# Strassen column tiles in a hybrid encoder trunk: ACT's and DVE's programs held in a written order, weight forms cast six products ahead

## The chip, the core and the metric

The kernel runs on one core of one Trainium2 chip. The metric is device time in microseconds, the median of repeated runs; one further execution was profiled. TensorE (PE) multiplies matrices, ScalarE (ACT) copies, rounds and evaluates functions, VectorE (DVE) adds and multiplies element by element, GpSimd (POOL) does a little of the rest, and SyncE (SP) issues the transfers from HBM. Each engine has a program of its own and runs it in order; semaphores tie them together.

## The reference

Two layers, 512 tokens of width 1024, float32. Each layer is a SwiGLU feed-forward block, a three-branch token mixer and a second SwiGLU block, each between RMSNorms, with residuals:

```python
def swiglu_ffn(h, w_gate, w_up, w_down):
    return (jax.nn.silu(h @ w_gate) * (h @ w_up)) @ w_down
...
for l in range(DEPTH):          # DEPTH = 2, D_MODEL = 1024, D_FF = 2816
    h = rms_norm(x, norm_pre[l, 0])
    x = x + 0.5 * rms_norm(swiglu_ffn(h, ffn1_w_gate[l], ffn1_w_up[l], ffn1_w_down[l]), norm_post[l, 0])
    h = rms_norm(x, norm_pre[l, 1])
    m = hybrid_mixer(h, ...)
    x = x + rms_norm(m, norm_post[l, 1])
    h = rms_norm(x, norm_pre[l, 2])
    x = x + 0.5 * rms_norm(swiglu_ffn(h, ffn2_w_gate[l], ffn2_w_up[l], ffn2_w_down[l]), norm_post[l, 2])
```

The change lies in the gate and up projections of the feed-forward blocks, so it is met four times in a run.

## The kernel before

**Precision.** A float32 operand is split into a high part, rounded by ACT to the matmul's format (a cast, `whi` for weights), and a low part, which DVE makes by subtracting (`wlo`). Each product of two operands is three matmuls: high by high, high by low, low by high.

**A feed-forward block** (`ffn`) has d_ff = 22 column tiles of 128. Tiles 0 and 1 are computed by tokens (bank `pf`) and turned, tile 2 in the plain way: `pg` and `pu` are its gate and up projections, DVE's product into `hid[2]` (L450) ends it. Meanwhile `forms.finish` splits the forms T1 to T4 of the activations. Tiles 3 to 21, 19 of them, go through `unit`: the gate and up columns of one tile are the two columns of a 2x2 block product (contraction halves by token halves) that is done by Strassen's scheme in Winograd's form with seven products instead of eight. Then `out_proj` multiplies by `w_down`.

**One tile.** The raw weights are four blocks of 128 x 512 in a buffer `raw` of five places (three such buffers); place 4 and in turn places 1, 0 and 2 are overwritten by four DVE sums (`add`, L348). The seven weight forms are cast and their low parts subtracted, two neighbouring forms by one DVE instruction where they can be paired. `whi` and `wlo` are rings of five buffers of two forms each. A product is 12 matmuls of 256 columns: 4 contraction chunks by 3. In order, with the bank each adds into:

| product | weight form | activation form | bank | afterwards |
|---|---|---|---|---|
| 0 | A11 | B11 | A | ACT copies A to p1 (L372) |
| 1 | S3 | T3 | C | ACT copies C to p7 (L380) |
| 2 | S2 | T2 | A | ACT copies A to u2 (L382) |
| 3 | A12 | B21 | B | DVE adds B and p1 into hid (L348) |
| 4 | S1 | T1 | A | ACT copies A to u4 (L392) |
| 5 | A22 | T4 | C | DVE subtracts u2 and u4 (L394, L395) |
| 6 | S4 | B22 | A | Silu of hid and of A (L399, L400), product into hid (L401) |

Bank A runs on through products 0, 2, 4 and 6, so each of them must wait until ACT has copied what the last one left there; between two of them lies one product into another bank.

**What sets the order.** TensorE's instructions are held in the order in which they are written (`mm` calls `tc.keep_in_program_order`). Everything on ACT, DVE and SP is placed by a scheduler, which fills each engine's program by what it reckons will be ready, the earlier written first; it can therefore move work of a later tile, of the forms or of the down projection ahead of what is written before it. The two Silus and the last product of a tile are written, by the argument `before`, after the third product of the next one.

Of the kernel before, what the change touches and what calls it, by code (L numbers as in the profile page):

```python
# [8 lines left out]
F32 = mybir.dt.float32  # L9
F32R = mybir.dt.float32r  # L10
AF = mybir.ActivationFunctionType
ALU = mybir.AluOpType

P = 128
D = 1024
# [4 lines left out]
NF = DFF // P  # L20
# [21 lines left out]
def kernel(  # L42
# [9 lines left out]
    nc = tc.nc  # L52
# [5 lines left out]
    wp = ctx.enter_context(tc.tile_pool(name="wp", bufs=5))  # L58
    tp = ctx.enter_context(tc.tile_pool(name="tp", bufs=1))
    gp = ctx.enter_context(tc.tile_pool(name="gp", bufs=2))  # L60
# [4 lines left out]
    def mm(*a, **k):  # L65
        tc.keep_in_program_order(nc.tensor.matmul(*a, **k))  # L66

    def transpose(*a):
        tc.keep_in_program_order(nc.tensor.transpose(*a))

    def slot(name, dt=F32, tag="t"):
        return tp.tile([P, 512], dt, tag=tag, name=name, bufs=SLOTS[tag])

    def bank(n, tag="pb"):
        return psp.tile([P, 512], F32, tag=tag, name=n, bufs=BANKS[tag])
# [9 lines left out]
    for c in range(2):  # L85
        blk = strict[:, c * CHUNK:(c + 1) * CHUNK]
        r = slice(c * CHUNK, (c + 1) * CHUNK)
# [68 lines left out]
    def load_kcols(w2d, c0, width):  # L156

        nk = 1024 // width
        v = lambda r: r.rearrange("p (k c) -> p k c", c=width)
        out_ = []  # L160
        for k0 in range(0, KC, nk):
            hi, lo = load_w([(v, w2d[k0 * P:(k0 + nk) * P, c0:c0 + width].rearrange("(k p) c -> p k c", p=P))], 1024)
            out_ += [(v(hi)[:, k], v(lo)[:, k]) for k in range(nk)]
        return out_
# [111 lines left out]
    class Forms:  # L276


        def __init__(self):
            self.first = []  # L280
            self.raw = None
            self.parts = {}
# [28 lines left out]
            for n, k0, t0 in (("B11", 0, 0), ("B21", 4, 0), ("B22", 4, 256)):  # L311
                self.parts[n] = [(xh[:, k0 + k, t0:t0 + 256], xl[:, k0 + k, t0:t0 + 256]) for k in range(4)]

    class Ring:


        def __init__(self):
            self.n = 0

        def put(self, src):  # L320

            two = len(src.shape) == 3
            if self.n % 2 == 0:
                self.hi, self.lo = (wp.tile([P, 1024], F32R, tag=t, name=t).rearrange("p (f c) -> p f c", f=2)
                                    for t in ("whi", "wlo"))
            h = self.n % 2
            assert not (two and h)
            self.n += 2 if two else 1
            f = slice(0, 2) if two else slice(h, h + 1)
            src = src if two else src.unsqueeze(1)  # L330
            for j in range(f.start, f.stop):
                nc.scalar.copy(self.hi[:, j], src[:, j - f.start])  # L332
            nc.vector.tensor_tensor(self.lo[:, f], src, self.hi[:, f].bitcast(F32), op=ALU.subtract)  # L333
            v = lambda t: t.rearrange("p (k c) -> p k c", c=P)
            r = [(v(self.hi[:, j]), v(self.lo[:, j])) for j in range(f.start, f.stop)]
            return r if two else r[0]

    H0, H1 = slice(0, 256), slice(256, 512)

    def unit(w0, w1, c0, forms, ring, h, before):  # L340


        r = wp.tile([P, 5, 512], F32, tag="raw", name="raw", bufs=3)
        for w, q0 in ((w0, 0), (w1, 1)):
            for j in range(2):
                nc.sync.dma_start(r[:, q0 + 2 * j].rearrange("p (k c) -> p k c", c=P),  # L346
                                  w[j * 512:(j + 1) * 512, c0:c0 + P].rearrange("(k p) c -> p k c", p=P))
        add = lambda o, a, b: nc.vector.tensor_tensor(o, a, b, op=ALU.add)  # L348
        add(r[:, 4], r[:, 1], r[:, 3])
        add(r[:, 1], r[:, 1], r[:, 0])  # L350
        A, B, C = bank("A"), bank("B"), bank("C")

        def product(w, n, ps, first):
            wh, wl = w
            for k, (fh, fl) in enumerate(forms.parts[n]):
                for j, (a, b) in enumerate(((wh, fh), (wh, fl), (wl, fh))):
                    mm(ps[:, H0], a[:, k], b, start=(first and k == 0 and j == 0), stop=False, skip_group_check=True)

        cp = gp.tile([P, D], F32, tag="g", name="cp")
        p1, p7, u2, u4 = (cp[:, j * 256:(j + 1) * 256] for j in range(4))  # L360
        put = ring.put
        even = ring.n % 2 == 0
        if even:
            a11, s3 = put(r[:, 0:2])
            add(r[:, 0], r[:, 4], r[:, 0])
            s2, a12 = put(r[:, 0:3:2])
        else:
            a11 = put(r[:, 0])
            add(r[:, 0], r[:, 4], r[:, 0])
            s2, s3 = put(r[:, 0:2])  # L370
        product(a11, "B11", A, True)
        nc.scalar.copy(p1, A[:, H0])  # L372
        if even:
            add(r[:, 2], r[:, 2], r[:, 0])
            a22, s1 = put(r[:, 3:5])
        else:
            a12, s1 = put(r[:, 2:5:2])
            add(r[:, 2], r[:, 2], r[:, 0])
        product(s3, "T3", C, True)
        nc.scalar.copy(p7, C[:, H0])  # L380
        product(s2, "T2", A, False)
        nc.scalar.copy(u2, A[:, H0])  # L382
        if before is not None:
            before()
        if even:
            s4 = put(r[:, 2])
        else:
            s4, a22 = put(r[:, 2:4])
        product(a12, "B21", B, True)
        add(h[:, H0], B[:, H0], p1)  # L390
        product(s1, "T1", A, False)
        nc.scalar.copy(u4, A[:, H0])  # L392
        product(a22, "T4", C, False)
        nc.vector.tensor_tensor(u2, C[:, H0], u2, op=ALU.subtract)  # L394
        nc.vector.tensor_tensor(u4, p7, u4, op=ALU.subtract)  # L395
        product(s4, "B22", A, False)

        def after():
            nc.scalar.activation(h[:, H0], h[:, H0], AF.Silu)  # L399
            nc.scalar.activation(h[:, H1], A[:, H0], AF.Silu)  # L400
            nc.vector.tensor_tensor(h, cp[:, 512:1024], h, op=ALU.mult)  # L401

        return after


    def ffn_weights(wg, wu):
# [5 lines left out]
    def ffn(wg, wu, wd, weights, forms, arrive, finish, upcoming, early, late, begin):  # L412

        if begin is None:
            wgt, wut = weights
        else:
            wgt = load_kcols(wg, 0, 256)
            begin(0)
            wut = load_kcols(wu, 0, 256)
            begin(1)  # L420
            arrive[0]()
        hk = []
        for i in range(NT):
            pf = bank("pf", "pb")
            mm_tok(pf[:, 0:256], i, wgt)
            if i + 1 < NT:
                arrive[i + 1]()
            mm_tok(pf[:, 256:512], i, wut, first=False)
            h = slot("ht", tag="s")
            nc.scalar.activation(h[:, 0:256], pf[:, 0:256], AF.Silu)  # L430
            nc.vector.tensor_tensor(h[:, 0:256], pf[:, 256:512], h[:, 0:256], op=ALU.mult)
            hk.append(h)
        hid = [None] * NF
        ring = Ring()

        def turn(f):
            pt = bank("pth", "pa")
            for i in range(NT):
                transpose(pt[:, i * P:(i + 1) * P], hk[i][:, f * P:(f + 1) * P], ident)
            hid[f] = slot("hid", tag="q")  # L440
            nc.scalar.copy(hid[f], pt)

        pg = proj_cols(wg, 2 * P, "pg")
        turn(0)
        turn(1)
        forms.finish()
        pu = proj_cols(wu, 2 * P, "pu")
        hid[2] = slot("hid")
        nc.scalar.activation(hid[2], pg, AF.Silu)
        nc.vector.tensor_tensor(hid[2], pu, hid[2], op=ALU.mult)  # L450
        spare.clear()
        last = None
        for f in range(3, NF):
            hid[f] = slot("hid", tag="t" if f < 18 else "q")
            last = unit(wg, wu, f * P, forms, ring, hid[f], last)
        last()
        late()

        def stat(f):
            sh, sl = slot("sh", F32R, "s"), slot("sl", F32R, "s")  # L460
            split(sh, sl, hid[f])
            return sh, sl

        return out_proj(wd, NF, stat, TAIL, finish, upcoming, early)
# [507 lines left out]
    g0 = load_g(norm_pre[0, 0])  # L972
    forms = form0 = Forms()
    arrive = [pre_norm(0, g0, forms=forms)]

    def begin(n):
        if n == 0:
            load_x(1)
            arrive.append(pre_norm(1, g0, forms=form0))
        else:  # L980
            load_x(2)
            load_x(3)
            arrive.extend(pre_norm(i, g0, forms=form0) for i in (2, 3))
# [3 lines left out]
    for idx, (l, s) in enumerate(subs):  # L987
# [10 lines left out]
        here, forms = forms, Forms() if s != 0 else None  # L998
# [11 lines left out]
        if idx + 1 < len(subs):  # L1010
            l1, s1 = subs[idx + 1]
# [39 lines left out]
```

## Time and profile before

| | us |
|---|---|
| runs shown: median of 3 | 2421.8 |
| lowest, highest | 2421.22, 2428.5 |
| profiled execution, its own time | 2428.07 |
| its span, first to last instruction | 2426.4 |
| PE busy | 2361.9 (97%) |
| DVE busy | 1620.8 (67%) |
| ACT busy | 1123.7 (46%) |
| mean granted TensorE clock | 0.997 |

How to read the profile's lines. A group's line gives source line, engine, operation, what is written from what, shape and count, then busy us and mean ns of one, then the engine's idle time ahead of the group and what ended it. A line of waits gives who waited for whom, the total in us, how many times, and the longest. A timeline's line gives start and duration in us, and in brackets the idle time before it and its releaser. A window's line gives each engine's busy time in a stretch, the granted clock and the share of the DMA engines. Matmuls are pipelined: 0.28 us is the modelled passage of one of 256 columns, while the next starts sooner. Most matmuls and nearly all casts go through one-line helpers, so the names (`A<-xh,whi`) tell more than the lines.

### The profile page before, as it was taken

What the parts mean: (1) busy time and instruction counts of PE and PEld (TensorE: products, weight loads), DVE (VectorE), ACT (ScalarE), POOL (GpSimd) and SP (SyncE); (2) the same over time, 40 slices, a digit from 0 to 9 for tenths busy, and PEclk for the clock granted to TensorE, in tenths of its full rate; (3) what the DMA queues carried; (4) which work ended last, traced back from release to release, by engine and by line L of the source; (5) the groups of instructions that cost most, each with busy time, mean ns of one, the idle gap of its engine ahead of it and who ended that gap; (6) DMA issues with size and microseconds to landing.
All of it is one profiled execution on the core that took longest, in us unless ns stands there. A gap on an engine that the chain in (4) does not pass through costs nothing. (4 is left out here: it accounts for less than half of the span.)

```text
span 2426.4 us, 35901 instructions
## 1 busy us (share of the span) xinstructions
PE 2361.9 (97%) x14264; PEld 2100.7 (87%) x14264; DVE 1620.8 (67%) x2329; ACT 1123.7 (46%) x2148; POOL 176.3 (7%) x287
## 2 busy tenths in 40 slices
PE   8999999999999999999999999999999999999998
PEld 7999888887888899998899998888878888999987
DVE  7777436859965497774387774378599644877733
ACT  6555426644323365553365553366333334555522
POOL 0000002201011100000000000012010211000000
PEclk9999999999999999999999999999999999999999
DMA  5333423231333233333233333241313332333331
GB/s 167 105 88 105 137 89 97 70 92 53 106 91 101 79 87 98 95 112 131 70 88 101 92 114 130 70 114 54 107 53 105 87 104 71 96 96 96 124 102 45
DMA packets 307160, 231.74 MB, mean 96 GB/s; under 512 B 11722, under 2 KB 284140, under 8 KB 306992
## 3 DMA queue, kind: packets, MB, share of 16 engines
q1 hardware_dynamic: 306992, 229.46, 31.9%
q8 instruction: 111, 1.82, 0.3%
q14 instruction: 57, 0.47, 0.1%
HBM read 227.32 MB, written 2.10 MB: 95 GB/s over the span
## 5 line engine op out<-in xcount | busy, mean ns | idle before, releaser
L106 DVE TENSOR_TENSOR wlo<-raw,whi 128x1024 fp32r<-128x1024 f32 (+1 forms) x266 | 333.6, 1258 | 236.1 <-ACT whi L105 229.0
L105 ACT CAST whi<-raw 128x1024 fp32r<-128x1024 f32 (+1 forms) x266 | 278.1, 1046 | 397.2 <-PE gate L66 122.6
L332 ACT CAST whi<-raw 128x512 fp32r<-128x512 f32 x532 | 323.8, 620 | 237.0 <-PE A L66 102.0
L333 DVE TENSOR_TENSOR wlo<-raw,whi 128x1024 fp32r<-128x1024 f32 (+1 forms) x304 | 330.5, 1087 | 68.7 <-ACT whi L332 65.3
L348 DVE TENSOR_TENSOR raw<-raw 128x512 f32<-128x512 f32 x304 | 203.8, 688 | 121.2 <-DMA raw<-in_ffn_w_up_dram 118.5
L66 PE MATMUL o<-whi,sh 128*128 128x512 f32 x704 | 274.2, 389 | 0.0
L66 PE MATMUL o<-wlo,sh 128*128 128x512 f32 x704 | 273.9, 389 | 0.0
L66 PE MATMUL o<-whi,sl 128*128 128x512 f32 x704 | 273.9, 389 | 0.0
L66 PE MATMUL A<-xh,whi 128*128 128x256 f32 x608 | 176.5, 290 | 43.8 <-ACT cp L392 43.7
L106 DVE TENSOR_TENSOR sl<-hid,sh 128x512 fp32r<-128x512 f32 x88 | 60.4, 690 | 193.8 <-ACT sh L105 193.8
L66 PE MATMUL A<-xh,wlo 128*128 128x256 f32 x608 | 173.4, 285 | 0.0
L66 PE MATMUL A<-xl,whi 128*128 128x256 f32 x608 | 173.4, 285 | 0.0
L641 DVE SCALAR_TENSOR_TENSOR y<-u,cw,y 128x511 f32<-128x511 f32 (+14 forms) x240 | 164.3, 747 | 0.0
L105 ACT CAST sh<-hid 128x512 fp32r<-128x512 f32 x88 | 54.5, 624 | 233.3 <-PE o L66 232.4
L66 PEld LDWEIGHTS A<-xh,whi 128*128 128x128 f32 x608 | 117.8, 194 | 50.1 <-ACT cp L392 49.8
L66 PEld LDWEIGHTS o<-whi,sl 128*128 128x128 f32 x704 | 132.1, 188 | 27.5
L66 PEld LDWEIGHTS o<-wlo,sh 128*128 128x128 f32 x704 | 132.2, 188 | 27.3
L66 PEld LDWEIGHTS o<-whi,sh 128*128 128x128 f32 x704 | 132.2, 188 | 27.1
L66 PE MATMUL gate<-xh,whi 128*128 128x512 f32 x384 | 151.3, 394 | 0.0
L66 PE MATMUL gate<-xl,whi 128*128 128x512 f32 x384 | 149.6, 390 | 0.0
L66 PE MATMUL gate<-xh,wlo 128*128 128x512 f32 x384 | 149.5, 389 | 0.0
L193 POOL TENSOR_TENSOR rs<-ms,mhalf 128x1 f32<-128x1 f32 x48 | 31.0, 646 | 1510.3 <-DVE ms L191 1510.3
(280 smaller groups left out, 6231.3 us busy)
## 6 DMA issues: line engine op xcount, KB each, us to landing
raw<-in_w_in_dram SPq DMA_DIRECT2D x108, 512.0 KB, 4.3
raw<-in_ffn_w_down_dram SPq DMA_DIRECT2D x88, 512.0 KB, 4.4
raw<-in_ffn_w_gate_dram SPq DMA_DIRECT2D x152, 256.0 KB, 3.3
raw<-in_ffn_w_up_dram SPq DMA_DIRECT2D x152, 256.0 KB, 4.5
raw<-in_w_branch_dram SPq DMA_DIRECT2D x24, 512.0 KB, 3.9
raw<-in_w_out_dram SPq DMA_DIRECT2D x16, 512.0 KB, 4.4
raw<-in_ffn_w_gate_dram SPq DMA_DIRECT2D x12, 512.0 KB, 5.3
raw<-in_ffn_w_up_dram SPq DMA_DIRECT2D x12, 512.0 KB, 4.1
```

What stands on the lines that cost most here:

```text
L66: tc.keep_in_program_order(nc.tensor.matmul(*a, **k))
L105: nc.scalar.copy(hi, src)
L106: nc.vector.tensor_tensor(lo, src, hi.bitcast(F32), op=ALU.subtract)
L193: nc.gpsimd.tensor_tensor(rs, ms, mhalf[:, 0:1], op=ALU.pow)
L332: nc.scalar.copy(self.hi[:, j], src[:, j - f.start])
L333: nc.vector.tensor_tensor(self.lo[:, f], src, self.hi[:, f].bitcast(F32), op=ALU.subtract)
L348: add = lambda o, a, b: nc.vector.tensor_tensor(o, a, b, op=ALU.add)
L641: nc.vector.scalar_tensor_tensor(y[:, back:], u[:, :S - back], cw[:, c, j:j + 1], y[:, back:], op0=ALU.mult, op1=ALU.add)
```

## The change

`unit` and its helper `Ring` are replaced by `block_tiles`, which writes the 19 tiles as one sequence of 133 products. A step `g` holds, in this order: on ACT the copies or Silus after product g-1 (`taken`); on PE product g; on DVE the sums and on ACT the cast for product g+6, then on DVE its low part (`prepare`; a pair's low part comes with the second form); on DVE what follows product g-1 (`summed`). Six steps with only `prepare` stand ahead of product 0. Each instruction on ACT and DVE is passed to `tc.keep_in_program_order`, which puts it behind the instruction that was traced last on its engine; loads on SP aren't held. The raw weights of tile u+2 are asked for where the first form of tile u+1 is prepared. The forms keep to the ring of five buffers, and pairs never cross a tile's end: an even tile has the pairs (0,1), (2,3), (4,5) and 6 alone, an odd one 0 alone and (1,2), (3,4), (5,6). Where the second form of a pair lies before the first in `raw`, both are addressed in reverse. The slots for `hid` are all named ahead of the sequence.

```diff
-    def unit(w0, w1, c0, forms, ring, h, before):
...
+    PRODUCTS = (("B11", 0), ("T3", 2), ("T2", 0), ("B21", 1), ("T1", 0), ("T4", 2), ("B22", 0))
+
+    PLACES = (0, 1, 0, 2, 4, 3, 2)
+    AHEAD = 6
+
+    def block_tiles(w0, w1, fs, forms, hid):
+
+        pin = tc.keep_in_program_order
+        copy = lambda o, i: pin(nc.scalar.copy(o, i))
+        silu = lambda o, i: pin(nc.scalar.activation(o, i, AF.Silu))
+        tt = lambda o, a, b, op: pin(nc.vector.tensor_tensor(o, a, b, op=op))
...
+        def low(g0, g1):
+
+            hi, lo = ring[g0 // 2]
+            q0, q1 = PLACES[g0 % 7], PLACES[g1 % 7]
+            r, h = raw[g0 // 7], g0 % 2
+            if g0 == g1:
+                sub(lo[:, h], r[:, q0], hi[:, h].bitcast(F32))
+            elif q0 < q1:
+                sub(lo, r[:, q0:q1 + 1:q1 - q0], hi.bitcast(F32))
+            else:
+                sub(lo[:, ::-1], r[:, q1:q0 + 1:q0 - q1], hi[:, ::-1].bitcast(F32))
+
+        def prepare(g):
+
+            u, j = divmod(g, 7)
+            r = raw[u]
+            if j == 0:
+                add(r[:, 4], r[:, 1], r[:, 3])
+                add(r[:, 1], r[:, 1], r[:, 0])
+            if j == 2:
+                add(r[:, 0], r[:, 4], r[:, 0])
+            if j == 5:
+                add(r[:, 2], r[:, 2], r[:, 0])
...
+            copy(ring[g // 2][0][:, g % 2], r[:, PLACES[j]])
+            if g % 2 and j:
+                low(g - 1, g)
+            elif g % 2 or j == 6:
+                low(g, g)
...
+        def taken(g):
...
+            if j == 0:
+                copy(p1, A[:, H0])
...
+            if j == 4:
+                copy(u4, A[:, H0])
+            if j == 6:
+                silu(h[:, H0], h[:, H0])
+                silu(h[:, H1], A[:, H0])
+
+        def summed(g):
...
+            if j == 3:
+                add(h[:, H0], B[:, H0], p1)
+            if j == 5:
+                sub(u2, C[:, H0], u2)
+                sub(u4, p7, u4)
+            if j == 6:
+                tt(h, cps[u][:, 512:1024], h, ALU.mult)
+
+        for g in range(-AHEAD, n + 1):
+            f = g + AHEAD
+            if f % 7 == 0 and f < n:
+                if f == 0:
+                    load(0)
+                if f // 7 + 1 < len(fs):
+                    load(f // 7 + 1)
+            if 0 < g:
+                taken(g - 1)
+            if 0 <= g < n:
+                product(g)
+            if f < n:
+                prepare(f)
+            if 0 < g:
+                summed(g - 1)
...
         spare.clear()
-        last = None
         for f in range(3, NF):
             hid[f] = slot("hid", tag="t" if f < 18 else "q")
-            last = unit(wg, wu, f * P, forms, ring, hid[f], last)
-        last()
+        block_tiles(wg, wu, list(range(3, NF)), forms, hid)
         late()
```

More of the change, by code (lines that the diff above doesn't have):

```diff
@@ L312, in finish @@
                 self.parts[n] = [(xh[:, k0 + k, t0:t0 + 256], xl[:, k0 + k, t0:t0 + 256]) for k in range(4)]
[L314 to L336, printed above, removed]
@@ L338 @@
-    H0, H1 = slice(0, 256), slice(256, 512)
-    def unit(w0, w1, c0, forms, ring, h, before):
[L343 to L403, printed above, removed]
@@ new lines, with load, product, parts @@
+    H0, H1 = slice(0, 256), slice(256, 512)
+    PRODUCTS = (("B11", 0), ("T3", 2), ("T2", 0), ("B21", 1), ("T1", 0), ("T4", 2), ("B22", 0))
[6 more added lines that the diff above has]
+        tt = lambda o, a, b, op: pin(nc.vector.tensor_tensor(o, a, b, op=op))
+        add = lambda o, a, b: tt(o, a, b, ALU.add)
+        sub = lambda o, a, b: tt(o, a, b, ALU.subtract)
+        n = 7 * len(fs)
+        raw, banks, cps, ring = {}, {}, {}, {}
+        def load(u):
+            r = wp.tile([P, 5, 512], F32, tag="raw", name="raw", bufs=3)
+            for w, q0 in ((w0, 0), (w1, 1)):
+                for j in range(2):
+                    nc.sync.dma_start(r[:, q0 + 2 * j].rearrange("p (k c) -> p k c", c=P),
+                                      w[j * 512:(j + 1) * 512, fs[u] * P:(fs[u] + 1) * P]
+                                      .rearrange("(k p) c -> p k c", p=P))
+            raw[u] = r
+        def low(g0, g1):
[18 more added lines that the diff above has]
+                add(r[:, 2], r[:, 2], r[:, 0])
+            if g % 2 == 0:
+                ring[g // 2] = [wp.tile([P, 1024], F32R, tag=t, name=t).rearrange("p (f c) -> p f c", f=2)
+                                for t in ("whi", "wlo")]
+            copy(ring[g // 2][0][:, g % 2], r[:, PLACES[j]])
[3 more added lines that the diff above has]
+                low(g, g)
+        def product(g):
+            u, j = divmod(g, 7)
+            name, b = PRODUCTS[j]
+            if j == 0:
+                banks[u] = [bank(x) for x in "ABC"]
+                cps[u] = gp.tile([P, D], F32, tag="g", name="cp")
+            ps = banks[u][b][:, H0]
+            hi, lo = (t[:, g % 2].rearrange("p (k c) -> p k c", c=P) for t in ring[g // 2])
+            first = j in (0, 1, 3)
+            for k, (fh, fl) in enumerate(forms.parts[name]):
+                for m, (a, b_) in enumerate(((hi, fh), (hi, fl), (lo, fh))):
+                    mm(ps, a[:, k], b_, start=(first and k == 0 and m == 0), stop=False, skip_group_check=True)
+        def parts(u):
+            cp = cps[u]
+            return [cp[:, x * 256:(x + 1) * 256] for x in range(4)], hid[fs[u]], banks[u]
+        def taken(g):
+            u, j = divmod(g, 7)
+            (p1, p7, u2, u4), h, (A, B, C) = parts(u)
+            if j == 0:
+                copy(p1, A[:, H0])
+            if j == 1:
+                copy(p7, C[:, H0])
+            if j == 2:
+                copy(u2, A[:, H0])
+            if j == 4:
[4 more added lines that the diff above has]
+        def summed(g):
+            u, j = divmod(g, 7)
+            (p1, p7, u2, u4), h, (A, B, C) = parts(u)
+            if j == 3:
[20 more added lines that the diff above has]
+                summed(g - 1)
@@ L433, in ffn @@
         hid = [None] * NF
-        ring = Ring()
         def turn(f):
```

## The prediction

> **What bounds the kernel now.** I read the page's busy lines first, then the list of waits, then the windows of the four Strassen stages, then the timeline of one stall and of one stage start.
>
> ```profile
> PE 2361.9 (97%) x14264; PEld 2100.7 (87%) x14264; DVE 1620.8 (67%) x2329; ACT 1123.7 (46%) x2148; POOL 176.3 (7%) x287
> ```
> ```profile
> DVE raw L348 <- DMA raw<-in_ffn_w_up_dram: 118.5, 65, 3.1
> ACT hid L399 <- DVE hid L348: 89.7, 56, 3.0
> PE A L66 <- ACT cp L392: 43.7, 28, 2.2
> ```
> ```profile
> core 0: us, PE busy (x) PEld busy (x) DVE busy (x) ACT busy (x) POOL busy (x), PEclk, DMA share, GB/s
> 52.40:258.40 206.00, 195.48 (x1598) 193.52 (x1596) 155.46 (x223) 115.71 (x248) 0.00 (x0) 0.99 0.34 101
> 890.80:1096.40 205.60, 193.61 (x1598) 191.96 (x1597) 155.22 (x224) 116.05 (x248) 0.00 (x0) 1.00 0.35 102
> 1255.10:1459.20 204.10, 193.63 (x1597) 191.89 (x1596) 155.04 (x223) 116.09 (x248) 0.00 (x0) 1.00 0.35 102
> 2094.30:2300.20 205.90, 195.03 (x1597) 193.37 (x1597) 155.59 (x224) 115.91 (x248) 0.00 (x0) 0.99 0.35 102
> sum 821.60, PE 777.75 PEld 770.74 DVE 621.30 ACT 463.75 POOL 0.00; mean PE 194.44 PEld 192.68 DVE 155.33 ACT 115.94 POOL 0.00
> ```
>
> TensorE is the bound nearly everywhere; its largest wait in the whole run is 43.7 us, on the copy of u4 (L392), in the stages that the change rewrites. Now one stall, first TensorE:
>
> ```profile
> 80.97 0.28 PE L66 MATMUL C<-T4l,whi 128*128 128x256 f32 x1
> 81.09 0.28 PE L66 MATMUL C<-T4h,wlo 128*128 128x256 f32 x1
> 82.66 0.39 PE L66 MATMUL A<-xh,whi 128*128 128x256 f32 x1 [1.29 <-ACT cp L392]
> 82.88 0.28 PE L66 MATMUL A<-xl,whi 128*128 128x256 f32 x1
> ```
>
> Matmuls start every 0.12 us, so a tile of 84 takes 10.08 us and a stage of 19 tiles 1596 x 0.12 = 191.5 us; four take 766.1 where the windows sum to 821.6. So 55.5 us are lost. The stall begins at 81.21 and ends at 82.66 (1.45), and the second matmul comes 0.10 late: 0.26 more than the row's 1.29. So 28 stalls are 43.7 + 28 x 0.26 = 51.0 of the 55.5. Who is late, on DVE and ACT:
>
> ```profile
> 78.19 1.42 DVE L348 TENSOR_TENSOR raw<-raw 128x512 f32<-128x512 f32 x2 [2.73 <-DMA raw<-in_ffn_w_up_dram]
> 79.53 1.22 DVE L333 TENSOR_TENSOR wlo<-raw,whi 128x1024 fp32r<-128x1024 f32 x1
> 80.66 0.42 DVE L348 TENSOR_TENSOR hid<-B,cp 128x256 f32<-128x256 f32 x1
> 81.00 0.68 DVE L348 TENSOR_TENSOR raw<-raw 128x512 f32<-128x512 f32 x1
> 82.36 1.23 DVE L333 TENSOR_TENSOR wlo<-raw,whi 128x1024 fp32r<-128x1024 f32 x1 [0.68 <-ACT whi L332]
> ```
> ```profile
> 81.11 0.42 ACT L399 ACTIVATE hid<-hid 128x256 f32<-128x256 f32 x1 [2.04 <-DVE hid L348]
> 81.71 0.62 ACT L332 CAST whi<-raw 128x512 fp32r<-128x512 f32 x1 [0.18 <-DVE raw L348]
> 82.24 0.37 ACT L392 COPY cp<-A 128x256 f32<-128x256 f32 x1
> 82.50 0.62 ACT L332 CAST whi<-raw 128x512 fp32r<-128x512 f32 x1
> ```
>
> DVE stands 2.73 us before weight sums for a later tile whose transfer has not landed; the sum into hid is queued behind it, ACT's Silu waits for that, a cast waits for another sum, and u4's copy, whose data were ready long before, comes last. It is a fault of the order on the two engines, not of their load. The rest of the 55.5 is mostly two stretches at half clock (below) and small gaps.
>
> **The change, part by part.** (a) *Same work.* Matmuls, casts, sums and transfers stay in number and size: per tile 4 weight sums, 7 casts, 3 paired and 1 single low part. Some paired subtractions read their halves in reverse. No row shows a reversed pair; a contiguous one takes 1.22 us, bounds zero and, as two singles of 0.60, nothing either. I take zero.
>
> (b) *Weights six products ahead.* The low part of product 6 of a tile is now cast while the tile's product 0 runs, so the raw buffer comes free about 8.6 us earlier and the load of the tile three on has more than a tile to land. The 118.5 us of DVE waits on transfers go; the transfers keep to SP's queue, with nothing new ahead of them.
>
> (c) *The copies out of PSUM first in each step.* u4's copy, queued in the step behind product T1, stands behind casts of earlier steps alone. Does that hold at full pace? I walked the written order for all 19 tiles, with these prices:
>
> ```profile
> L333 DVE TENSOR_TENSOR wlo<-raw,whi 128x1024 fp32r<-128x1024 f32 x54 | 66.0, 1222 | 18.6 <-ACT whi L332 18.1
> L348 DVE TENSOR_TENSOR raw<-raw 128x512 f32<-128x512 f32 x67 | 44.8, 688 | 27.2 <-DMA raw<-in_ffn_w_up_dram 26.6
> L394 DVE TENSOR_TENSOR cp<-C,cp 128x256 f32<-128x256 f32 x19 | 7.9, 418 | 0.4 <-PE C L66 0.4
> ```
> ```profile
> 84.17 1.22 DVE L333 TENSOR_TENSOR wlo<-raw,whi 128x1024 fp32r<-128x1024 f32 x1
> 85.31 0.69 DVE L401 TENSOR_TENSOR hid<-cp,hid 128x512 f32<-128x512 f32 x1
> 85.91 0.69 DVE L348 TENSOR_TENSOR raw<-raw 128x512 f32<-128x512 f32 x1
> ```
>
> Back to back, DVE starts its next after 1.14 us for a pair (84.17 to 85.31), 0.60 for 512 columns, 0.33 for 256; ACT after 0.53 for a cast (81.71 to 82.24) and 0.26 for a copy. DVE's tile is 4 x 0.60 + 3 x 1.14 + 0.60 + 3 x 0.33 + 0.60 = 8.0 of 10.08 us, ACT's about 5.5. A handoff costs 0.03 us (81.00 + 0.68 to ACT at 81.71; 81.71 + 0.62 to DVE at 82.36), so does a wait of DVE for its own result (two sums of 0.69 in 1.42), and ACT or DVE starts 0.20 us after a product's last matmul slot. In the walk the weights lie ready 3.7 us early or more. The copies do not. The tightest chain is in an odd tile, where product 0 starts at 0, product k at 1.44 k, and the forms of the next tile are made. The last Silu of the tile before:
>
> ```profile
> L400 ACT ACTIVATE hid<-A 128x256 f32<-128x256 f32 x18 | 6.9, 381 | 6.5 <-PE A L66 6.5
> ```
>
> It runs 0.20 to 0.58; behind it the cast of S4 0.48 to 1.10; DVE's low pair 1.13 to 2.36, the product into hid 2.28 to 2.97, the sums of r4 and r1 2.88 to 3.57 and 3.61 to 4.30; the cast of S3 4.33 to 4.95, its low pair 4.98 to 6.21, r0's sum 6.24 to 6.93, the casts of S2 and A12 6.97 to 8.11; and only then u4's copy, 8.01 to 8.38, though product 4 ended at 7.20. Product 6 starts at 8.64: 0.2 us to spare. In even tiles u2's copy has the same 0.2, behind the cast of S3. Each tile's chain starts anew from TensorE's own end, so nothing piles up. I take no stall in steady state, by a hair. Below that price there is nothing; above, a stage of the old order took 206.0 us for 19 tiles, 21.7 us for two.
>
> (d) *The start of a stage.* Each held instruction goes behind whatever was traced last on its engine. For DVE that is the product into hid[2] (L450), which needs all of pu:
>
> ```profile
> 39.45 1.22 DVE L333 TENSOR_TENSOR wlo<-raw,whi 128x1024 fp32r<-128x1024 f32 x1
> 40.70 0.69 DVE L348 TENSOR_TENSOR raw<-raw 128x512 f32<-128x512 f32 x1
> ...
> 52.62 0.69 DVE L450 TENSOR_TENSOR hid<-pu,hid 128x512 f32<-128x512 f32 x1 [0.69 <-PE pu L66]
> ```
> ```profile
> 52.19 0.39 PE L66 MATMUL pu<-xh,wlo 128*128 128x512 f32 x1
> 52.42 0.28 PE L66 MATMUL A<-xh,whi 128*128 128x256 f32 x1
> ```
>
> Before, the first tile's low parts and sums ran from 39 us on, during pf, pg and pu, and the first product followed pu without a gap. Now DVE can't touch them until pu is done. Let 0 be that first slot (52.42). L450 runs 0.20 to 0.89; r4's sum starts 0.81, r1's runs 1.53 to 2.22; ACT's cast of S3 2.25 to 2.87; the low pair of products 0 and 1 2.90 to 4.13. The third matmul of product 0 needs it, starts at 4.18 instead of 0.24, and TensorE loses 3.94 us. Products 0 and 1 then end at 4.18 + 10 x 0.12 + 1.44 = 6.82. Product 2 goes into bank A and needs p1 copied out, and in ACT's program that copy stands behind the casts of all of products 0 to 6: DVE's r0 4.16 to 4.85, casts 4.88 to 6.02, low pair 6.05 to 7.28, r2 7.31 to 8.00, cast of S4 8.03 to 8.65, copy 8.55 to 8.92, product 2 at 8.97: 2.15 us more. Product 4 waits 0.2, restarts take 0.1 each: 6.5 us a stage, 26 us in four. Bounds: 0, if something still lets the sums go first, and 8, if the handoffs take three times 0.03. I take 6.5: the names in the code leave no choice of order.
>
> ```profile
> L105 ACT CAST whi<-raw 128x1024 fp32r<-128x1024 f32 (+1 forms) x266 | 278.1, 1046 | 397.2 <-PE gate L66 122.6
> ```
>
> (e) *The end of a stage.* The first casts for the down projection are not held and fill gaps as before (TensorE waits nothing there now). Raw buffers come free earlier, so I take 0; if the cover failed, one cast of 1.05 and its low part of 1.22 would show, 2.3 us a stage.
>
> (f) *Clock.* Two stalls were followed by half rate, and so was one stretch in the mixer:
>
> ```profile
> 212.64:216.06 3.42, 1.67 (x14) 1.47 (x13) 2.74 (x5) 2.35 (x5) 0.00 (x0) 1.00 0.00 0
> 216.06:219.47 3.41, 3.41 (x18) 3.41 (x17) 2.93 (x5) 0.38 (x1) 0.00 (x0) 0.50 0.63 180
> ```
> ```profile
> 1762.30:1769.12 6.82, 5.98 (x12) 4.08 (x13) 5.82 (x11) 1.86 (x4) 0.00 (x0) 0.50 0.00 0
> 2257.23:2260.64 3.41, 3.41 (x18) 3.41 (x17) 3.00 (x5) 1.06 (x3) 0.00 (x0) 0.50 0.44 126
> ```
>
> A stretch of 3.41 us with TensorE half idle (1.67 busy) was followed by 3.41 us at 0.50, which costs up to 1.7 us. The new start stall of 3.94 us would do this at every stage; but products 0 and 1 need 2.64 us at full rate, 5.1 at half, and have from 4.18 to 8.97 before p1's copy lets product 2 go: at most 0.3 us shows. I take nothing. [...]
>
> **Sum.** On the profiled execution's 2428.07 us (span 2426.4): -55.5 + 26 = 2398.6. It stands 6.3 us above the median of 2421.8; its three half-rate stretches, up to 3.41 x 2 = 6.8 us, are of that size, so I read the median as without them and take only 52.5 us as there to gain. 2421.8 - 52.5 + 26 = 2395, and 1 us for small stalls at the thin margin of (c): **2396 us**.
>
> **Rivals.**
> *Start covered.* If the first tile's sums still run during pu, all stalls go: 2421.8 - 52.5 = 2369. For it speaks that ACT and DVE have room there; against it that L450 is the last DVE instruction traced before the held ones.
>
> *The clock after the start stall* isn't hidden: 4 x 1.7 = 6.8 us more, 2403. For it speaks the row at 216, against it the second wait, which covers it. [...]
>
> *Slower: the copies of u2 and u4 fall behind.* The margin is 0.2 us. If two tiles take DVE and ACT more than TensorE's 20.16 us, the excess is paid 38 times. Breaking even needs 26 / 38 = 0.68 us; with the 21.7 us of the old order, 1.5 in excess is 57 us: 2453. Six handoffs lie in the chain of (c), so it would need each to cost some 0.12 us instead of 0.03: 2 x (6 x 0.09 - 0.2) = 0.68. For it speaks the thin margin; against it that the handoffs in the rows are all 0.03. With a third of that excess the time is near 2415, no change.
>
> *Loads remain late*, so that DVE still stands as at 78.19: nothing gained and the start paid, 2421.8 + 26 = 2448. Against it: (b).
>
> **How the numbers follow.** Forecast 0.62 (its own range 2385 to 2412), clock 0.10, start covered 0.10, copies behind 0.14 (about half of it slower, the rest shared), loads late 0.04. A difference under 0.3%, 7.3 us, can't be told from none here. Faster: 0.62 + 0.10 + 0.10 less a little for the forecast's tail = 0.80; same 0.08; slower 0.12. The range runs from full cover, 2370, to half of the copies' slow case, 2430.
>
> **What would show it.** The 43.7 us wait on u4's copy gone; DVE's wait on the up-weights' transfers near zero; each stage's windows at about 198 us; at each start a wait of TensorE of some 4 us for a low part and one of 2 us for p1's copy, with L450 ahead of the first sums. I am wrong if the stages stay above 203 us, through many short waits on u2's and u4's copies, or if they start without a gap.

## The result, and the profile after

The change makes the kernel faster, by 1.05%, close to the forecast of 2396.

| us | before | after |
|---|---|---|
| median | 2423.35 (4 executions) | 2398.64 (4 executions) |
| lowest, highest | 2421.22, 2428.5 | 2397.77, 2399.89 |
| ratio, 95% interval | | 0.9895 [0.9878, 0.9913] |
| profiled execution, its own time | 2428.07 | 2397.77 |
| its span | 2426.4 | 2396.1 |
| mean granted clock | 0.997 | 0.993 |

The page's busy lines of the kernel after; each engine has as many instructions as before:

```profile
PE 2360.0 (98%) x14264; PEld 2104.1 (88%) x14264; DVE 1631.2 (68%) x2329; ACT 1118.0 (47%) x2148; POOL 175.9 (7%) x287
```

Its list of waits for TensorE alone (who waited for whom, total us, times, longest us):

```profile
PE A L66 <- DVE wlo L326: 15.1, 4, 3.8
...
PE A L66 <- ACT cp L324: 0.4, 1, 0.4
```

The 28 stalls on u4's copy (43.7 us) are gone. In their place stand four waits of 3.8 us for a low part, one at the start of each stage. DVE's wait for the up-weights' transfers, 118.5 us before, is no longer in the list. The windows of the four stages, the first and the third with the sum (each some 0.1 us wider than its stage):

```profile
51.80:249.80 198.00, 194.22 (x1599) 193.94 (x1598) 166.70 (x236) 117.92 (x254) 0.00 (x0) 0.98 0.36 108
...
1241.40:1439.40 198.00, 193.78 (x1598) 193.20 (x1597) 166.67 (x236) 117.89 (x254) 0.00 (x0) 0.99 0.37 108
...
sum 792.30, PE 776.73 PEld 775.28 DVE 666.71 ACT 471.54 POOL 0.00; mean PE 194.18 PEld 193.82 DVE 166.68 ACT 117.89 POOL 0.00
```

821.6 us became 792.3: 29.3 of the 30.3 us between the two profiled executions. Every stage now takes nearly the same, some 6.4 us over the 191.5 of a gapless one (the fourth 6.7). Those 6.4 us lie at its start. First TensorE's timeline of the first start, then DVE's, then ACT's:

```profile
51.67 0.39 PE L66 MATMUL pu<-xh,wlo 128*128 128x512 f32 x1
51.90 0.28 PE L66 MATMUL A<-xh,whi 128*128 128x256 f32 x1
52.01 0.28 PE L66 MATMUL A<-xl,whi 128*128 128x256 f32 x1
56.08 0.58 PE L66 MATMUL A<-xh,wlo 128*128 128x256 f32 x1 [3.78 <-DVE wlo L326]
...
60.72 0.41 PE L66 MATMUL C<-T3h,wlo 128*128 128x256 f32 x1
60.94 0.49 PE L66 MATMUL A<-T2h,whi 128*128 128x256 f32 x1
```
```profile
52.10 0.69 DVE L478 TENSOR_TENSOR hid<-pu,hid 128x512 f32<-128x512 f32 x1 [2.49 <-PE pu L66]
52.70 1.41 DVE L326 TENSOR_TENSOR raw<-raw 128x512 f32<-128x512 f32 x2
54.80 1.23 DVE L326 TENSOR_TENSOR wlo<-raw,whi 128x1024 fp32r<-128x1024 f32 x1 [0.68 <-ACT whi L324]
```
```profile
59.94 0.62 ACT L324 CAST whi<-raw 128x512 fp32r<-128x512 f32 x1 [0.98 <-DVE raw L326]
60.46 0.36 ACT L324 COPY cp<-A 128x256 f32<-128x256 f32 x1
```

DVE idles 2.49 us until pu is done, multiplies into hid[2] (L450 before, L478 now), and only then makes the first sums. The low part for the third matmul of product 0 starts at 54.80, and TensorE stands from 52.13 to 56.08. p1's copy, behind the casts of all of products 0 to 6 on ACT, starts 8.56 us after the first slot, and product 2 9.04 after it.

### The profile page after: what moved, and what is told of

Same layout as the page of the kernel before. It is cut to its first block, busy times and chain, and to the rows that moved or that the text cites. A ratio compares the mean times of both kernels' runs of the same rounds, so it can differ in the third digit from the quotient of the medians.

```text
span 2396.1 us, 35810 instructions
## 1 busy us (share of the span) xinstructions
PE 2360.0 (98%) x14264; PEld 2104.1 (88%) x14264; DVE 1631.2 (68%) x2329; ACT 1118.0 (47%) x2148; POOL 175.9 (7%) x287
## 4 chain that ended last, share of the span: by engine, by line
PE 96%; DVE 2%; ACT 1%; issue 0%; POOL 0%; DMA 0%; SPq 0%; DVEq 0%; POOLq 0%; ACTq 0%
PE o L66 23%; PE A L66 18%; PE gate L66 11%; PE C L66 9%; PE pb L66 5%; PE B L66 5%; PE pf L66 4%; PE pa L66 2%; PE gr L66 2%; PE q L66 2%; PE gv L66 2%; PE k L66 2%; PE pgl L66 2%; PE pv L66 2%; PE pu L66 1%; PE gk L66 1%
## 5 line engine op out<-in xcount | busy, mean ns | idle before, releaser
L324 ACT CAST whi<-raw 128x512 fp32r<-128x512 f32 x532 | 314.2, 619 | 187.3 <-DVE raw L326 187.3
L326 DVE TENSOR_TENSOR raw<-raw 128x512 f32<-128x512 f32 x304 | 209.2, 688 | 6.6
L66 PEld LDWEIGHTS A<-xh,wlo 128*128 128x128 f32 x608 | 118.8, 195 | 15.9 <-DVE wlo L326 15.9
```

The source lines that it names most:

```text
L324: copy = lambda o, i: pin(nc.scalar.copy(o, i))
L326: tt = lambda o, a, b, op: pin(nc.vector.tensor_tensor(o, a, b, op=op))
```

## The experiments

Times are medians beside the kernel before on the same chip; ratios are to that kernel.

### 1. The sums of the first tile ahead of hid[2]'s product

`block_tiles` becomes a generator that stops ahead of product 0, so that its six steps with only `prepare` are traced before the two instructions on hid[2].

```diff
         for g in range(-AHEAD, n + 1):
+            if g == 0:
+                yield
...
         pu = proj_cols(wu, 2 * P, "pu")
+        tiles = block_tiles(wg, wu, list(range(3, NF)), forms, hid)
+        next(tiles)
         hid[2] = slot("hid")
...
-        block_tiles(wg, wu, list(range(3, NF)), forms, hid)
+        for _ in tiles:
+            pass
```

> The six steps that only prepare are traced ahead of the product into hid[2], so the held instructions of the first tile no longer stand behind it. Theory (the order at the stage's start costs all that is left): each stage loses the 3.9 us wait, the half-rate stretch after it and p1's late copy, 6.4 us in all, so four stages give 25 us: 2373 us, ratio to before 0.979, stage windows near 192 us. Rival (the first tile is short of something else at its start, of its raw weights or of ring buffers): part of the wait comes back with a DMA or PE as releaser, 2380 to 2395 us.

Measured: 2371.56 us (2368.57 to 2373.14), before 2425.21, ratio 0.9778 [0.9758, 0.9798]. The windows of its stages:

```profile
51.78:243.30 191.52, 191.52 (x1598) 191.52 (x1597) 160.51 (x229) 114.57 (x248) 0.00 (x0) 1.00 0.38 111
...
sum 766.08, PE 766.08 PEld 766.07 DVE 642.06 ACT 458.27 POOL 0.00; mean PE 191.52 PEld 191.52 DVE 160.52 ACT 114.57 POOL 0.00
```

Each stage takes exactly 1596 x 0.12 us with TensorE busy throughout. So the start is all that the change still loses, some 27 us (2398.64 - 2371.56), and the order in the middle of a stage costs nothing. This version beats both kernels.

### 2. Weights four products ahead

With a lead of 4, p1's copy stands behind fewer casts, while the first wait stays as it is.

```diff
-    AHEAD = 6
+    AHEAD = 4
```

> Forms are cast four products ahead instead of six, so p1's first copy stands behind the casts of products 0 to 4 and is done some 1.5 us before product 2 could start. The 3.9 us wait at the start stays. Theory A (after that wait the half-rate clock alone sets the pace, p1's copy is hidden under it): the stages stay within 0.6 us of 197.9, 2396 to 2399 us. Theory B (p1's copy is what ends the loss, the clock is hidden under it): 2.1 us less a stage, 2390 us. Both expect no stall in the steady state, since the weights would still be 0.8 us early.

Measured: 2397.96 us (2395.16 to 2398.26), ratio 0.9886 [0.9866, 0.9906]: the kernel after's time. ACT's and TensorE's timelines of the first start, whose first slot is at 51.21, and the sum of its stages' windows:

```profile
57.66 0.36 ACT L324 COPY cp<-A 128x256 f32<-128x256 f32 x1
```
```profile
59.38 0.41 PE L66 MATMUL A<-T2h,whi 128*128 128x256 f32 x1
59.59 0.41 PE L66 MATMUL A<-T2l,whi 128*128 128x256 f32 x1
```
```profile
sum 790.24, PE 774.14 PEld 772.44 DVE 649.51 ACT 462.44 POOL 0.00; mean PE 193.54 PEld 193.11 DVE 162.38 ACT 115.61 POOL 0.00
```

The copy ends at 58.02, over a microsecond ahead of need, and still product 2 starts at 59.38, because TensorE runs at half rate (slots 0.21 apart, as in the kernel after where the granted clock is 0.50). Two causes of nearly equal length lie side by side at this start: take away the copy's lateness and the clock sets the pace. In this execution, the fastest of the four, the slots are 0.21 apart from 56.60 to 59.81 at this start, each stage's window shows a granted clock of 0.99 where three of the kernel after's four show 0.98, and a start loses some 5.5 us instead of 6.4. Of that, 0.4 to 0.7 us a stage come back, as a wait for u2's copy in the last tile:

```profile
PE A L66 <- ACT cp L324: 1.0, 4, 0.4
```

Between the start and that tile, six products of lead aren't needed: with four, too, DVE waits for no transfer and TensorE for nothing.

### 3. The same lead, nothing held

```diff
-        pin = tc.keep_in_program_order
+        pin = lambda i: i
```

> The same program text, with its lead of six products, but no instruction of ACT and DVE is held to the written order. Theory (the gain is the order on the two engines): the scheduler moves the first tile's sums ahead of hid[2]'s product again and later weight sums ahead of the sum into hid, the waits on u4's copy return, some 40 us of them, the wait at the start goes: 2420 to 2425 us. Rival (the gain is the lead, through earlier loads): the stalls stay away and the start is free, near 2373 us.

Measured: 2424.99 us (2421.12 to 2430.57), ratio 1.0005 [0.9992, 1.0018]: no gain is left. Its waits, in total and on TensorE:

```profile
DVE raw L326 <- DMA raw<-in_ffn_w_up_dram: 115.2, 63, 3.5
...
PE A L66 <- ACT cp L324: 40.5, 29, 2.2
```

These are the old waits, although the code has the lead of six. The timelines show why. For the same tile, the sixth of the first stage, this is SP's queue and DVE with nothing held, and then both in the kernel after:

```profile
71.64 1.06 SPq L336 DMA_DIRECT2D raw<-in_ffn_w_up_dram  x2
```
```profile
77.98 1.42 DVE L326 TENSOR_TENSOR raw<-raw 128x512 f32<-128x512 f32 x2 [3.02 <-DMA raw<-in_ffn_w_up_dram]
```
```profile
82.09 1.05 SPq L336 DMA_DIRECT2D raw<-in_ffn_w_up_dram  x2
```
```profile
101.78 1.41 DVE L326 TENSOR_TENSOR raw<-raw 128x512 f32<-128x512 f32 x2
```

Left free, the scheduler puts the tile's sums right behind its load, and DVE stands 3.02 us until the data land, 27 us before the tile's product 0 (105.41). Held, the load even goes out 10 us later, but the sums come 20 us after it and wait for nothing; product 0 starts at 108.68, 7 us on. So the old order made the sums too early, not too late.

### 4. r4's sum twice per tile

This adds 0.60 us to the chain ahead of the copies of u2 and u4, as the rival of the slower case would have it.

```diff
                 add(r[:, 4], r[:, 1], r[:, 3])
+                add(r[:, 4], r[:, 1], r[:, 3])
                 add(r[:, 1], r[:, 1], r[:, 0])
```

> r4's sum is made twice in every tile (the result is the same), which puts 0.6 to 0.7 us more of DVE work into the chain ahead of u2's and u4's copies. DVE then has 8.7 us of work in a tile of 10.08. Theory (the copies have only 0.2 us to spare): some 0.6 us a tile shows as waits of TensorE on copies, 10 to 13 us a stage, 40 to 50 us in all: 2440 to 2450 us. Rival (DVE's load decides, and that has room): nothing but 0.7 us at each start, 2401 us.

Measured: 2451.37 us (2451.14 to 2452.5), ratio 1.011 [1.009, 1.0129], 52.7 more than the kernel after. TensorE's waits for copies, and its timeline at the three late products of a pair of tiles:

```profile
PE A L66 <- ACT cp L324: 19.7, 38, 0.7
```
```profile
97.69 0.39 PE L66 MATMUL A<-T1h,whi 128*128 128x256 f32 x1
97.91 0.28 PE L66 MATMUL A<-T1l,whi 128*128 128x256 f32 x1
...
100.89 0.39 PE L66 MATMUL A<-xh,whi 128*128 128x256 f32 x1
...
108.85 0.39 PE L66 MATMUL A<-T1h,whi 128*128 128x256 f32 x1 [0.49 <-ACT cp L324]
```

Only 38 waits are listed, about one for each pair of tiles, though three products of a pair come late. The slots before these were at 97.34, 100.54 and 108.07, so with the 0.10 by which the next one lags the losses are 0.33, 0.33 and 0.76: 1.42 us a pair, 12.8 for the nine pairs of a stage. The first two are too short to be listed. The first wait of a stage is 0.7 us longer too (4.5 in the list of waits, 3.8 in the kernel after); four times 13.5 is 54, against the 52.7 measured. The expectation of 10 to 13 us a stage through late copies was right; the longer first waits put the time just above its 2440 to 2450. So the margin is as thin as the prediction had it, and the slower case was near: one more small instruction on DVE loses all the gain and more.

### 5 and 6. Only one engine held

Both stand on experiment 1. In one, ACT's instructions are left to the scheduler, in the other, DVE's.

```diff
-        copy = lambda o, i: pin(nc.scalar.copy(o, i))
-        silu = lambda o, i: pin(nc.scalar.activation(o, i, AF.Silu))
+        copy = lambda o, i: nc.scalar.copy(o, i)
+        silu = lambda o, i: nc.scalar.activation(o, i, AF.Silu)
```

> As the run with the first tile's sums ahead of hid[2]'s product (2371.6 us), but only DVE's instructions are held to the written order; ACT's casts, copies and Silus are placed by the scheduler. Theory (the stalls before came from DVE standing at sums whose transfer had not landed): DVE's waits on the up weights stay near zero and TensorE's waits on copies return little or not at all, 2372 to 2385 us. Rival (the copies need their held place on ACT): waits on u2's or u4's copy return in most tiles, 2395 us or more.

```diff
-        tt = lambda o, a, b, op: pin(nc.vector.tensor_tensor(o, a, b, op=op))
+        tt = lambda o, a, b, op: nc.vector.tensor_tensor(o, a, b, op=op)
```

> The other half: ACT's instructions are held to the written order, DVE's are placed by the scheduler, the first tile's sums free to go ahead. Theory (DVE's order is the cause): DVE again stands at later sums for their transfers and the waits on u4's copy come back, 2400 to 2425 us. Rival (ACT's order suffices): near 2372 us.

Measured: with DVE alone held 2372.43 us (2368.95 to 2373.71), ratio 0.9782 [0.9765, 0.9798], and no wait of TensorE on a copy: the same as with both. With ACT alone held 2381.82 (2381.56 to 2384.78), ratio 0.9825 [0.981, 0.9841]. The waits of that one, on DVE and on TensorE:

```profile
DVE raw L326 <- DMA raw<-in_ffn_w_up_dram: 54.8, 35, 3.5
...
DVE wlo L326 <- DMA raw<-in_ffn_w_gate_dram: 19.8, 22, 0.9
...
PE A L66 <- ACT cp L324: 4.8, 11, 0.8
```

DVE's order does it alone. ACT's alone is worth most of it too, which the expectation of 2400 to 2425 missed: DVE still stands 74.6 us before transfers, but with the copies placed ahead on ACT little of that reaches TensorE, and it costs 10 us, not 50.

### 7. Weights two products ahead

Again on experiment 1, with both engines held.

```diff
-    AHEAD = 6
+    AHEAD = 2
```

> As the run with the first tile's sums ahead, both engines held, but the forms are cast two products ahead instead of six. Theory (held in this order, the lead is what keeps the weights ahead): the low parts come 0.4 to 1.1 us late in about two products of five, some 34 us a stage by the same walk with the same prices, 2500 us, give or take 20, with low parts as releasers. Rival (the order alone does it, two products of lead, 2.9 us, are enough for a cast of 0.6 and a low part of 1.2): 2372 us.

Measured: 2525.35 us (2524.35 to 2526.51), ratio 1.0413 [1.0395, 1.0431]. TensorE's waits (those on bank B are as those on C):

```profile
PE A L66 <- DVE wlo L326: 65.5, 116, 1.0
PE C L66 <- DVE wlo L326: 20.3, 36, 0.6
```

In a fixed order the low parts now come too late for about one product in three (188 waits, 532 products). A stage takes 38.4 us more than in experiment 1 ((2525.35 - 2371.56) / 4) where the walk gave 34, and the time lies 5 us above the range expected. DVE waits for no transfer here either. A fixed order needs its lead: not for the transfers, but for the low parts.

## Why the prediction was right, point by point

**(a) Same work: as forecast.** The timings of all of DVE's low parts, singles and pairs, reversed ones among them (min, median, max in ns), in the kernel after:

```profile
L326 DVE TENSOR_TENSOR wlo<-raw,whi x304: 681/1224/1228, 54.8 to 2261.9; 128x1024 fp32r<-128x1024 f32 x116, 128x512 fp32r<-128x512 f32 x36
```

None takes over 1228, and a contiguous pair took 1222. A reversed pair costs nothing.

**(b) Transfer waits go: right in outcome, wrong in reason.** The prediction put it down to raw buffers coming free 8.6 us earlier through the lead. Measured against the tile that they are for, they come free later. This is SP's queue in the kernel before, with the load of the sixth tile, for which DVE's sums at 78.19 wait:

```profile
72.15 1.06 SPq L346 DMA_DIRECT2D raw<-in_ffn_w_up_dram  x2
```

That tile's product 0 starts at 106.28, 34 us later. In the kernel after the same load goes out at 82.09, 27 us before product 0 at 108.68. Experiment 3 has the lead and keeps 115.2 us of the waits, with its load (71.64) 34 us ahead of product 0, as in the kernel before; experiments 2 and 7 have leads of 4 and 2 in the held order, and no such waits. Of these, 2 runs the tiles at the full 10.08 us, so that it isn't a slower pace that gives the transfers time. What removes them is DVE's held order, in which a tile's sums come well after its load.

**(c) The copies hold by a hair: right.** An odd tile of the kernel after, ACT, DVE and TensorE; its product 0 starts at 88.52:

```profile
88.72 0.38 ACT L325 ACTIVATE hid<-A 128x256 f32<-128x256 f32 x1 [1.15 <-PE A L66]
89.00 0.61 ACT L324 CAST whi<-raw 128x512 fp32r<-128x512 f32 x1
...
92.83 0.62 ACT L324 CAST whi<-raw 128x512 fp32r<-128x512 f32 x1 [0.86 <-DVE raw L326]
...
96.57 0.37 ACT L324 COPY cp<-A 128x256 f32<-128x256 f32 x1
```
```profile
89.64 1.23 DVE L326 TENSOR_TENSOR wlo<-raw,whi 128x1024 fp32r<-128x1024 f32 x1 [0.27 <-ACT whi L324]
...
91.38 1.41 DVE L326 TENSOR_TENSOR raw<-raw 128x512 f32<-128x512 f32 x2
93.48 1.23 DVE L326 TENSOR_TENSOR wlo<-raw,whi 128x1024 fp32r<-128x1024 f32 x1 [0.69 <-ACT whi L324]
```
```profile
97.04 0.28 PE L66 MATMUL C<-T4h,wlo 128*128 128x256 f32 x1
97.16 0.28 PE L66 MATMUL A<-xh,whi 128*128 128x256 f32 x1
```

From 88.52 the Silu is at 0.20 (walk 0.20), the cast of S4 at 0.48 (0.48), the low pair at 1.12 (1.13), the cast of S3 at 4.31 (4.33) and u4's copy at 8.05 (8.01). It ends at 96.94, 0.22 us ahead of product 6 (0.2 forecast). The prices of the old timeline, handoffs of 0.03 included, held when chained over a dozen steps. Experiments 1 and 4 bound it: no stall with the margin, stalls in every pair of tiles once 0.60 is added.

**(d) The start of a stage: right.** First wait 3.95 us (3.94; 52.13 to 56.08, a matmul's slot being 0.12 after 52.01), p1's copy 8.56 after the first slot (8.55), product 2 at 9.04 (8.97), 6.4 us a stage (6.5). That L450's place is the cause, experiment 1 shows: moved behind the sums, all of it goes. Experiment 2 adds to it that the copy behind seven casts is not the only cause of the second part.

**(e) The end of a stage: as forecast**, no wait of TensorE for the down projection's casts is in the list.

**(f) The clock: right, and closer than the text made it.** Windows of the kernel after behind its four starts, cut where the granted clock is 0.50:

```profile
54.44:61.26 6.82, 5.18 (x24) 5.15 (x25) 5.19 (x6) 3.82 (x9) 0.00 (x0) 0.50 0.00 0
...
887.29:894.11 6.82, 5.04 (x23) 5.00 (x24) 5.04 (x6) 3.82 (x8) 0.00 (x0) 0.50 0.00 0
...
1245.69:1249.10 3.41, 3.38 (x16) 3.38 (x17) 2.16 (x3) 2.18 (x4) 0.00 (x0) 0.50 0.00 0
...
2075.13:2081.95 6.82, 6.08 (x28) 6.04 (x29) 5.55 (x7) 3.86 (x8) 0.00 (x0) 0.50 0.00 0
```

The granted clock falls to 0.50 at every start, as the prediction and its rival had it, and stays down longer than the 3.41 us assumed, in three of four cases for twice that. It still costs next to nothing, because p1's copy ends at 60.82 and product 1's last matmul starts at 60.72: whichever is later sets product 2, and they are 0.1 us apart. At the third start, where full rate came back at 1249.10, the copy, ending at 1250.47, alone set it (1250.53), with the 0.4 us wait of the list. At the fourth, half rate went on to 2081.95, into product 2 (from 2080.73), and the stage is 0.4 us longer, where the prediction allowed 0.3.

**The sum.** On the profiled execution it was 2398.6 against 2397.77. On the medians it was 2396 against 2398.64, and the term that failed is the base, not the change: 2421.8 of three executions was low (2425.21 of 13 later ones), and it was wrong to read the distance of the profiled execution to it as half-rate stretches missing from the others: eight of those 13 were granted a lower mean clock than its 0.997. From 2425.21 the stalls are worth 53.6 (experiment 1; 52.5 forecast) and the starts cost 27.1 (26): 2398.6. The extra microsecond for small stalls is not there.

**The rivals.** *Start covered* is experiment 1 (2371.56, 2369 forecast), not this change. *The copies behind* is experiment 4, one sum of 0.60 us a tile away. *Loads remain late* is experiment 3's picture, without the price of the start, since nothing is held there.

## What to carry to other kernels

An order written by hand pays in the middle of a stage and must be looked at again at its start: the first held instruction stands behind whatever was traced last on its engine, and here that one line's place cost half of the gain. Where an engine with room to spare stands before a transfer, look whether its work is too early rather than too late, and hold that engine alone: the other may not need it. When a walk leaves a fraction of a microsecond, add one small instruction to the chain and run it, and you know how near the edge is.

## What the runs showed of the hardware

At the four starts of the kernel after, half rate lasted 3.41 us once and 6.82 us three times. Its windows at the third and the fourth start, in stretches of 3.41 us; the third's stretch at half rate, 1245.69 to 1249.10, stands above:

```profile
1242.28:1245.69 3.41, 0.00 (x0) 0.00 (x0) 2.67 (x4) 0.62 (x1) 0.00 (x0) 1.00 0.00 0
...
1249.10:1252.51 3.41, 2.98 (x24) 2.77 (x24) 3.38 (x5) 1.69 (x4) 0.00 (x0) 1.00 0.01 3
```
```profile
2071.72:2075.13 3.41, 0.37 (x3) 0.17 (x1) 2.52 (x4) 0.62 (x1) 0.00 (x0) 1.00 0.00 0
2075.13:2078.54 3.41, 2.67 (x12) 2.67 (x13) 2.17 (x3) 1.96 (x4) 0.00 (x0) 0.50 0.00 0
2078.54:2081.95 3.41, 3.41 (x18) 3.38 (x17) 3.38 (x5) 1.90 (x5) 0.00 (x0) 0.50 0.00 0
```

At the third start TensorE does nothing in the stretch ahead of half rate (0.00 busy); the next is at half rate, TensorE is busy for 3.38 us of it, and behind it the rate is full again. At the fourth the stretch ahead of half rate has 0.37 us busy, and the stall reaches 0.7 us into the next, which then has only 2.67 of 3.41 us busy, and one more follows at half rate. At the first and the second start the stretch ahead of half rate has 1.27 and 1.41 us busy (51.02 to 54.44, 883.88 to 887.29), the first one at half rate 1.77 and 1.63, and a second follows there too. So the three stalls that went on after half rate had set in, by 1.64, 1.78 and 0.74 us, had 6.82 us of it, and the one that ended 0.03 us after it had 3.41. How idle a stretch must be for half rate to follow is not shown: behind the prediction's row with 1.67 us busy it followed, behind one of the kernel before with 1.68 (1369.77 to 1373.18) and one of the kernel after with 1.45 (10.07 to 13.48) it did not.
